# A diffusion-transformer layer on one core: two more 1 MB slots for streamed weights, and a 16-float load on another queue

## The chip, the core and the metric

The kernel runs on one core of one Trainium2 chip. The core has a matrix engine (PE), a vector engine (DVE), a scalar engine (ACT), GpSimd (POOL) and a sync engine (SP) that here only issues transfers; every engine works through its own list of instructions in order. 16 DMA engines move data between device memory and the on-chip buffer (SBUF), which matmuls read; matmul results go to PSUM. The metric is the time of the whole layer on the device in microseconds (us).

## The reference

One layer over 512 tokens of width 1024, in float32: modulated RMSNorm, a projection to gated-MLP and attention inputs, chunked spatial gating, windowed attention with a sink, a gated merge, an output projection, and then a mixture of 16 experts in which each expert picks its 64 tokens.

```python
m = jnp.maximum(jnp.max(logits, axis=-1, keepdims=True), sink_l)      # sink: 16 floats, one a head
denom = jnp.sum(p, axis=-1, keepdims=True) + jnp.exp(sink_l - m)
...
h2 = modulate(rmsnorm(x, norm2_g[l]), sh2, sc2)
aff = jax.nn.softmax(h2 @ w_router, axis=-1)
top_w, top_idx = lax.top_k(jnp.swapaxes(aff, 1, 2), 64)               # 64 tokens for each of 16 experts
xe = h2[top_idx]
y = (silu(xe @ w_gate) * (xe @ w_up)) @ w_down                        # 3 x 8 MB of weights an expert
x = x + g2 * scatter_add(y * top_w)
out = rmsnorm(x, final_g)
```

## The kernel before

Tokens lie on partitions in four tiles of 128. The source fixes the order on every engine (`manual_schedule`); a framework adds the waits. Large data lives in `NW` = 24 slots of 1 MB (`W()`, 128 partitions of 2048 floats); a new tile takes a slot whose last reader is done, and its writer waits for that reader. Small tiles are `S()` (6 of 512 floats a partition), PSUM tiles `B()` and `B2()`.

**The start** (lines 115 to 475). SP issues, in order: a table, `x`, parameter rows, the first half of `w_ada` in 8 transfers (`load_ada(0)`), the first piece of `w_in`, `ctx`, parameter rows, `load(1)` (1 MB), `load_ada(1)` (8 of 0.5 MB), and the mask and rotation table `tab` (line 409, 832 KB). SP keeps eight transfers under way, each on one of eight semaphores in turn: a transfer is issued when the one eight before it has landed. The attention sink (16 floats, to all partitions, 8 KB) is loaded on POOL's queue (line 133) and negated on DVE (line 134), the second instruction of DVE's list. DVE, ACT and PE then turn `x` by features (lines 400 to 404) and multiply the condition with `w_ada` (`mod_rows`, line 278); `mod_cols(0)` copies that result (DVE, line 284), turns it (PE, line 288) and makes scale and shift; `mod_x(0)` applies them (DVE line 303, ACT line 304), and the first products of the projection (`mm3`, lines 110 to 112) follow on PE.

**The middle** (to about 590 us) is a row of such products, attention and the merge. The sink is read there, from line 570 on.

**The experts.** Each expert's weights come in 24 pieces of 1 MB (8 gate, 8 up, 8 down), 384 in all, in one order (`stream`); `stream_to(n)` issues them up to number n. In the last projection it is called with 13 and 15, before the top-64 search with `ring[0]` = NW - 2 = 22 (two slots hold the residual rows `acc`), and then in `take(i)`, which allows pieces up to i + `ring[0]`. At the first expert's piece 8, `settle()` takes three slots out of the ring: two for the normed rows `xn` (ACT, line 1189) and one, `g2w`, for a gate row and transposed hidden values; from there on a piece goes to the slot that was freed 19 pieces earlier. For the first expert the rows are gathered from the raw rows `xacc` with a one-hot matrix that carries the norm's factor (`gather_first`); the others gather from `xn` (`gather`, line 1124). `up_half` does gate and up on PE (line 1211), `down` the rest (line 1250). The rows of the expert before are added to `xacc` in `up_half` after pieces 1 and 4 (`add_rows`, PE line 1265, DVE line 1272). After the last expert come the last additions, the norm and four stores.

Of the kernel before, what the change touches and what calls it, by code (L numbers as in the profile page):

```python
# [5 lines left out]
F32 = mybir.dt.float32  # L6
F32R = mybir.dt.float32r
AF = mybir.ActivationFunctionType
ALU = mybir.AluOpType
# [3 lines left out]
P = 128  # L13
D = 1024
T = 512
NT = 4
CT = 2
KD = 8
H = 16
G = 4  # L20
DH = 64
E = 16
# [1 line left out]
DE = 2048  # L24
EPS = 1e-6
NEG = -1e30
NW = 24

TAB_MASK = 0
TAB_C = 1152  # L30
# [40 lines left out]
def bc_rows(ap1d, n):  # L71
    return bass.AP(tensor=ap1d.tensor, offset=ap1d.offset, ap=[[0, P], [1, n]])


def layer(tc, I, out, dbg=None):
    nc = tc.nc
    pe, act, dve, gp, sp = nc.tensor, nc.scalar, nc.vector, nc.gpsimd, nc.sync
    from contextlib import ExitStack
    with ExitStack() as st:
        cp = st.enter_context(tc.tile_pool(name="cp", bufs=1))  # L80
        big = st.enter_context(tc.tile_pool(name="big", bufs=NW))
        sm = st.enter_context(tc.tile_pool(name="sm", bufs=6))
# [5 lines left out]
        def W(dt=F32):  # L88
            return big.tile([P, 2048], dt, name="w")

        def S(dt=F32):
            return sm.tile([P, 512], dt, name="s")

        def V(n=4):
            t = tiny.tile([P, 16], F32, name="v")
            return t[:, :n]

        def B(dt=F32):
            return psb.tile([P, 512], dt, name="b")

        def B2():
            return ps2.tile([P, 1024], F32, name="b2")
# [27 lines left out]
        vT = cp.tile([P, C_N], F32, name="vT")  # L130
        modT = cp.tile([P, 16, 2], F32, name="modT")
        sink = cp.tile([P, H], F32, name="sink")
        gp.dma_start(sink, bc_rows(I["attn_sink"][0], H))
        dve.tensor_scalar(sink, sink, -1.0, None, ALU.mult)


        win = I["w_in"][0]
# [75 lines left out]
        for i in range(2):  # L213
            for j in range(2):
                t = 2 * i + j
# [7 lines left out]
        def load_ada(h):  # L223

            for i in range(4):
                w = W()
                for j in range(2):
                    k = 2 * i + j
                    wv = w[:, j * D:(j + 1) * D].rearrange("p (m c) -> p m c", m=2)
                    src = I["w_ada"][0, k * P:(k + 1) * P, 0:2048].rearrange("p (m a c) -> a p m c", m=2, a=2)[h]  # L230
                    sp.dma_start(wv, src)
                ada[h, i] = w
# [38 lines left out]
        def mod_rows(h, i):  # L271

            if i == 0:
                pms[h] = b2m[:, :512] if h else B()
            for m in range(2):
                for j in range(2):
                    o = 32 * (2 * j + m)
                    pe.matmul(pms[h][o:o + 32, :], sT[:, 2 * i + j, :], ada[h, i][:, j * D + m * 512:j * D + (m + 1) * 512],
                              start=(i == 0), stop=(i == 3))
# [117 lines left out]
        for k in range(KD):  # L397
            p = B()
# [8 lines left out]
        load(1)  # L407
        load_ada(1)
        sp.dma_start(tab[:, :TAB_IOTA], I["tab"][:, :TAB_IOTA])

        mod_rows(0, 3)
        for _ in range(2):
# [272 lines left out]
        for a in range(2):  # L685
            p = B()
# [67 lines left out]
        sh2c, a2c, g2c = [cp.tile([P, KD], F32, name=n) for n in ("sh2c", "a2c", "g2c")]  # L754
# [56 lines left out]
                dve.tensor_tensor(wr, wr, a2c[:, :, None].to_broadcast([P, KD, E]), ALU.mult)  # L811
                dve.tensor_reduce(part, wt.rearrange("p k e -> p e k"), axis=AX.X, op=ALU.add)

        part = cp.tile([P, E], F32, name="part")

        def shift_logits():
            ones = S()[:, :P]
# [16 lines left out]
        for side in range(2):  # L834
            yh, yl = (yah, yal) if side == 0 else (ybh, ybl)
            for c in range(4):
# [5 lines left out]
                for u_ in range(4):  # L842
                    f = 2 * c + u_ % 2
                    wh, wl = tiles[i0 + u_]
                    p = B()
# [15 lines left out]
                    else:  # L861
                        z = zs[u_ - 2]
                        m = mA[f // 4][:, (f % 4) * T:(f % 4 + 1) * T]
# [29 lines left out]
        ew = {}  # L893
        ring = [NW - 2]
        issued = [0]
# [12 lines left out]
        xacc = lambda t: acc[t // 2][:, (t % 2) * D:(t % 2 + 1) * D]  # L908
        for t in range(NT):
            sp.dma_start(xacc(t), I["x"][0, t * P:(t + 1) * P, :])  # L910
        xnw = []
        xn = lambda t: xnw[t // 2][:, (t % 2) * D:(t % 2 + 1) * D]
        rstd2 = cp.tile([P, NT], F32, name="rstd2")
        aff = cp.tile([P, NT, E], F32, name="aff")
        def out_cols(t, c0, n, hooks):

            p = B()[:, :n]
            for k in range(KD):
                wh, wl = split_done[30 + c0 // 512 * 2 + k // 4]
                c = slice(c0 % 512, c0 % 512 + n)  # L920
                mm3(p, mgh(k)[:, t * P:(t + 1) * P], mgl(k)[:, t * P:(t + 1) * P], wh[:, k % 4, c], wl[:, k % 4, c],
                    k == 0, k == KD - 1)
                if k + 1 in hooks:
                    hooks[k + 1]()
            return p
# [35 lines left out]
                dve.tensor_copy(XT[t, c0][:, :n], p[:, :n])  # L961

        strips = {}
        pos = cp.tile([P, NT, E], F32, name="pos")
        fold = pos[:, 0]
        dve.tensor_reduce(fold, idt.rearrange("p (j c) -> p c j", j=4)[:, :E], axis=AX.X, op=ALU.add)

# [57 lines left out]
        for i, (t, c0, n) in enumerate(units):  # L1025
            before = units[i - 1] if i else None
# [3 lines left out]
            p = out_cols(t, c0, n, hooks)  # L1030
# [41 lines left out]
        def one_hot(e, scale=None):  # L1072
            oh = S()[:, :512].rearrange("p (t s) -> p t s", t=NT)
            for t in range(NT):
                o = oh[:, t].rearrange("p (h s) -> p h s", h=2)
                if scale is None:
                    dve.tensor_scalar(o, iota, pos[:, t, e:e + 1], None, ALU.is_equal)  # L1077
                else:
                    dve.tensor_scalar(o, iota, pos[:, t, e:e + 1], scale[:, t:t + 1], ALU.is_equal, ALU.mult)
            return oh  # L1080
# [36 lines left out]
                to_modulated(0, pt[a], ks, a * 256)  # L1117

        def gather(e):
            oh = one_hot(e)  # L1120
            p = B()
            for t in range(NT):
                for h in range(2):
                    pe.matmul(p[h * 64:(h + 1) * 64, :], oh[:, t, :64], xn(t)[:, h * 512:(h + 1) * 512],  # L1124
                              start=(t == 0), stop=(t == NT - 1))
            XE[e] = p, oh

        def gather_turn(e):
# [10 lines left out]
        def gather_rest(e):  # L1139

            xt, ohv = XE[e]
            if e == 0:
                ohv = one_hot(e)
            pw = B()
            for t in range(NT):
                pe.matmul(pw[:, :1], ohv[:, t], aff[:, t, e:e + 1], start=(t == 0), stop=(t == NT - 1))  # L1146
            tw = V(1)
            dve.tensor_copy(tw, pw[:, :1])
            pt_ = B()
            for t in range(NT):  # L1150
                pe.transpose(pt_[:, t * P:(t + 1) * P], ohv[:, t], idt)
            oht = S()
            act.activation(oht[:, :512], pt_, AF.Copy)
            XE[e] = (xt, tw, oht)

        g2w = []

        def diag_rows(cols, a, w):

            ones = S()[:, :w]  # L1160
            gp.memset(ones, 1.0)  # L1161
            dg = S()
            gp.tensor_tensor(dg.rearrange("p (k c) -> p k c", k=4), idt[:, None, :].to_broadcast([P, 4, P]),
                             cols[:, a * 4:a * 4 + 4, None].to_broadcast([P, 4, P]), ALU.mult)
            return ones, dg
# [9 lines left out]
        def spread_halves(o, cols):  # L1175

            p = B()
            for a in range(2):
                ones, dg = diag_rows(cols, a, 64)
                pe.matmul(p[a * 64:(a + 1) * 64, :], ones, dg, start=True, stop=True)  # L1180
            dve.tensor_copy(o, p)

        def settle():

            xnw.extend([W(), W()])
            g2w.append(W())
            ring[0] -= 3
            for t in range(NT):
                act.activation(xn(t), xacc(t), AF.Copy, scale=rstd2[:, t:t + 1])
            spread_halves(g2w[0][:, :512], g2c)  # L1190

        def take(i):
            if i == KD:
                settle()
            stream_to(i + ring[0])
            return ew.pop(i)

# [2 lines left out]
        def up_half(e, before):  # L1200
            xt = XE[e][0]
            pp_ = []
            for m in range(2):
                p = B2()
                pp_.append(p)
                for k in range(KD):
                    w = take(e * 24 + m * 8 + k)
                    x = xt[:, k % 4, k // 4, :]
                    for n in range(2):
                        for h in range(2):  # L1210
                            pe.matmul(p[h * 64:(h + 1) * 64, n * 512:(n + 1) * 512], x,  # L1211
                                      w[:, h * D + n * 512:h * D + (n + 1) * 512],
                                      start=(k == 0), stop=(k == KD - 1))
                    if before and m == 0 and k in (1, 4):
                        add_rows(*before, (0, 1) if k == 1 else (2, 3))
            hs = []
            for n in range(2):
                s = S()
                act.activation(s[:, :512], pp_[0][:, n * 512:(n + 1) * 512], AF.Silu)  # L1219
                dve.tensor_tensor(s[:, :512], s[:, :512], pp_[1][:, n * 512:(n + 1) * 512], ALU.mult)  # L1220
                hs.append(s)
            HT[e] = hs
# [45 lines left out]
        def add_rows(e, yw, ts):  # L1268
            ps = put_back(e, yw, ts)
            for (t, c), p in ps.items():  # L1270
                x = xacc(t)[:, c * 512:(c + 1) * 512]
                dve.tensor_tensor(x, x, p, ALU.add)  # L1272
# [67 lines left out]
```

## Time and profile before

| what | us |
|---|---|
| median of 3 runs (1558.88 to 1560.78) | 1559.96 |
| the profiled execution, its own time | 1560.64 |
| its span, first to last instruction | 1558.9 |
| PE busy | 1441.8 (92%) |
| DVE / ACT / POOL busy | 530.4 / 317.2 / 124.2 |
| bytes moved | 474.15 MB, mean 304 GB/s |

The profile shows one execution on a time axis that starts with its first instruction. A busy PE says little by itself, since matmuls are pipelined; what matters in a stretch is who waits for whom there.

### The profile page before, as it was taken

Reading aid. Unit: us, or ns where it says so; the run is one execution under the profiler, and the core shown is the slowest. Engines: PE = TensorE matmul, PEld = TensorE weight load, DVE = VectorE, ACT = ScalarE, POOL = GpSimd, SP = SyncE. Lnnn points to the kernel's source line nnn. Section 1 sums busy time; section 2 is a strip of 40 time slices with the busy share of each in tenths; the row PEclk is TensorE's granted clock in tenths of the full one; section 3 lists DMA queues with packets and bytes.
Section 4 is the critical chain, followed back from the end, with each engine's and each line's share of the span. In section 5 each row is a group of like instructions: output and inputs, shape, how many; then the busy total and the mean of one; then the engine's idle time right before and its main releaser. Section 6 shows DMA issues by size and latency. Waiting matters only on the chain.

```text
span 1558.9 us, 18259 instructions
## 1 busy us (share of the span) xinstructions
PE 1441.8 (92%) x7471; PEld 764.7 (49%) x7471; DVE 530.4 (34%) x1079; ACT 317.2 (20%) x605; POOL 124.2 (8%) x184
## 2 busy tenths in 40 slices
PE   5899999999999997999999999989989889889895
PEld 3687787788788884333333333323323323323221
DVE  4666555468664335112112121211211112112123
ACT  4456555533232331200000000000000000000002
POOL 2143322000000321000000000000000000000002
PEclk9999999999999998999999999999999999999998
DMA  9310000437762666999999999999999999999994
GB/s 330 127 55 28 28 28 28 136 106 251 254 174 82 240 246 273 374 412 420 420 419 420 420 420 419 419 420 420 420 420 419 420 419 419 420 419 419 420 420 183
DMA packets 99272, 474.15 MB, mean 304 GB/s; under 512 B 8842, under 2 KB 38770, under 8 KB 47986
## 3 DMA queue, kind: packets, MB, share of 16 engines
q1 hardware_dynamic: 99156, 472.97, 76.3%
q8 instruction: 59, 0.97, 0.3%
q0 software_dynamic: 32, 0.01, 0.1%
q14 instruction: 25, 0.20, 0.0%
HBM read 470.85 MB, written 2.10 MB: 303 GB/s over the span
## 4 chain that ended last, share of the span: by engine, by line
PE 73%; issue 14%; DMA 5%; DVE 5%; ACT 3%; SPq 0%; POOL 0%; POOLq 0%; ACTq 0%; DVEq 0%
PE b L1211 15%; PE b L1250 13%; PE b L110 8%; PE b L112 8%; PE b L111 8%; PE b L1265 4%; PE b L1124 4%; PE b L610 3%; PE b L617 2%; DMA w<-in_w_exp_up_dram 1%; DMA w<-in_w_exp_gate_dram 1%; DMA w<-in_w_exp_down_dram 1%; DVE s L1220 1%; PE b L1232 1%; PE b L1146 1%
## 5 line engine op out<-in xcount | busy, mean ns | idle before, releaser
L1211 PE MATMUL b<-w,s 128*64 128x512 f32 x2048 | 460.6, 596 | 28.8 <-DMA w<-in_w_exp_up_dram 28.8
L1211 PEld LDWEIGHTS b<-w,s 128*64 128x64 f32 x2048 | 139.0, 137 | 343.3 <-issue 256.6
L110 PE MATMUL b<-w 128*128 128x512 f32 (+1 forms) x720 | 257.2, 357 | 2.7 <-ACT w L304 2.7
L112 PE MATMUL b<-w 128*128 128x512 f32 (+1 forms) x720 | 247.6, 344 | 0.0
L111 PE MATMUL b<-w 128*128 128x512 f32 (+1 forms) x720 | 247.3, 344 | 0.0
L1250 PE MATMUL b<-w 128*64 128x512 f32 x1024 | 227.9, 596 | 2.7 <-DMA w<-in_w_exp_down_dram 2.5
L110 PEld LDWEIGHTS b<-w 128*128 128x128 f32 x720 | 136.7, 190 | 34.6 <-issue 11.4
L112 PEld LDWEIGHTS b<-w 128*128 128x128 f32 x720 | 136.5, 190 | 16.7 <-DVE w L308 0.4
L111 PEld LDWEIGHTS b<-w 128*128 128x128 f32 x720 | 136.9, 190 | 15.3 <-issue 0.2
L1250 PEld LDWEIGHTS b<-w 128*64 128x64 f32 x1024 | 70.2, 137 | 137.6 <-issue 128.6
L1220 DVE TENSOR_TENSOR s<-s,b 128x512 f32<-128x512 f32 x32 | 20.6, 684 | 312.3 <-issue 285.1
L1272 DVE TENSOR_TENSOR w<-w,b 128x512 f32<-128x512 f32 x128 | 79.5, 682 | 128.3 <-PE b L1265 128.3
L1219 ACT ACTIVATE s<-b 128x512 f32<-128x512 f32 x32 | 17.4, 594 | 343.3 <-PE b L1211 343.3
L107 POOL TENSOR_TENSOR w<-w 128x512 fp32r<-128x512 f32 x52 | 67.3, 1308 | 194.0 <-ACT w L106 185.7
L106 ACT ACTIVATE w<-w 128x512 fp32r<-128x512 f32 (+2 forms) x97 | 79.9, 848 | 8.5 <-DVE w L315 5.0
L1235 ACT ACTIVATE w<-b 128x512 f32<-128x512 f32 x16 | 9.6, 597 | 335.6 <-PE b L1232 335.6
L1124 PE MATMUL b<-w,s 128*64 128x512 f32 x240 | 54.8, 598 | 24.7 <-DVE s L1077 24.7
L1161 POOL MEMSET s<- 128x64 f32 (+1 forms) x4 | 0.7, 180 | 872.6 <-PE b L1135 850.2
L571 DVE CUSTOM_DVE_ANT_0 w<-b,w,sink 128x512 f32<-128x512 f32 (+1 forms) x64 | 51.5, 813 | 52.7 <-PE b L567 52.4
L1265 PE MATMUL b<-s 64*128 64x512 f32 x256 | 65.0, 616 | 1.8 <-DVE w L1272 1.0
L107 DVE TENSOR_TENSOR w<-w 128x1024 fp32r<-128x1024 f32 (+1 forms) x45 | 58.0, 1293 | 24.8 <-ACT w L106 24.8
L583 ACT ACTIVATE w<-w,v 128x513 f32<-128x513 f32 (+1 forms) x64 | 49.0, 769 | 0.0
(223 smaller groups left out, 1110.2 us busy)
## 6 DMA issues: line engine op xcount, KB each, us to landing
w<-in_w_exp_gate_dram SPq DMA_DIRECT2D x128, 1024.0 KB, 19.9
w<-in_w_exp_up_dram SPq DMA_DIRECT2D x128, 1024.0 KB, 19.9
w<-in_w_exp_down_dram SPq DMA_DIRECT2D x128, 1024.0 KB, 19.9
w<-in_w_in_dram SPq DMA_DIRECT2D x21, 1024.0 KB, 5.1
w<-in_w_ada_dram SPq DMA_DIRECT2D x16, 1024.0 KB, 5.0
w<-in_w_ada_dram SPq DMA_DIRECT2D x16, 512.0 KB, 6.0
w<-in_x_dram SPq DMA_DIRECT2D x8, 512.0 KB, 6.1
w<-in_w_proj_a_dram SPq DMA_DIRECT2D x4, 1024.0 KB, 5.2
```

The source lines that it names most:

```text
L106: act.activation(hi, raw, AF.Copy)
L107: eng.tensor_tensor(lo, raw, hi.bitcast(F32), ALU.subtract)
L110: pe.matmul(o, sh, mh, start=first, stop=False)
L111: pe.matmul(o, sh, ml, start=False, stop=False)
L112: pe.matmul(o, sl, mh, start=False, stop=last)
L571: dve.tensor_tensor_reduce(s[:, :w_], p[:, 256:256 + w_], mask[:, c0:c0 + w_], -1.0, sk, ALU.add, ALU.min, mx[:, r:r + 1])
L583: act.activation(sm_t[r][:, :w_], sm_t[r][:, :w_], AF.Exp, bias=mx[:, r:r + 1], scale=-1.0, accum_out=den[:, r:r + 1])
L1124: pe.matmul(p[h * 64:(h + 1) * 64, :], oh[:, t, :64], xn(t)[:, h * 512:(h + 1) * 512], start=(t == 0), stop=(t == NT - 1))
L1211: pe.matmul(p[h * 64:(h + 1) * 64, n * 512:(n + 1) * 512], x, w[:, h * D + n * 512:h * D + (n + 1) * 512], start=(k == 0), stop=(k == KD - 1))
L1250: pe.matmul(y[c * 64:(c + 1) * 64, :], hT[n][:, i % 2, j, h, :], w[:, j * D + c * 512:j * D + (c + 1) * 512], start=(i == 0 and j == 0), s ...
L1265: pe.matmul(ps[t, c], XE[e][2][r, t * P:(t + 1) * P], yw[r, :], start=True, stop=True)
L1272: dve.tensor_tensor(x, x, p, ALU.add)
```

## The change

The buffer of big slots grows from 24 to 26; room comes from a smaller DMA scratch area of GpSimd (64 bytes) and from `part`, which becomes a piece of `pos`. GpSimd issues no transfer any more: the sink is loaded by SP, behind `tab`, and its negation stands at that place of the source. The three slots of `settle` are taken in two steps: `g2w` at piece 8, as before, and the two for `xn` at piece 26, the third of the second expert. So the second expert too is gathered from `xacc` with a scaled one-hot matrix, and `gather_rest(1)` makes a plain one. `add_rows` comes after pieces 3 and 6, so that the rows are copied before they are changed.

```diff
-NW = 24
+NW = 26
...
-        gp.dma_start(sink, bc_rows(I["attn_sink"][0], H))
-        dve.tensor_scalar(sink, sink, -1.0, None, ALU.mult)
...
         load_ada(1)
         sp.dma_start(tab[:, :TAB_IOTA], I["tab"][:, :TAB_IOTA])
+        sp.dma_start(sink, bc_rows(I["attn_sink"][0], H))
+        dve.tensor_scalar(sink, sink, -1.0, None, ALU.mult)
 
         mod_rows(0, 3)
...
-        part = cp.tile([P, E], F32, name="part")
+        pos = cp.tile([P, NT, E], F32, name="pos")
+        part = pos[:, 1]
...
         def gather(e):
-            oh = one_hot(e)
+
+            oh = one_hot(e, None if xnw else rstd2)
+            rows_ = xn if xnw else xacc
...
-                    pe.matmul(p[h * 64:(h + 1) * 64, :], oh[:, t, :64], xn(t)[:, h * 512:(h + 1) * 512],
+                    pe.matmul(p[h * 64:(h + 1) * 64, :], oh[:, t, :64], rows_(t)[:, h * 512:(h + 1) * 512],
                               start=(t == 0), stop=(t == NT - 1))
+            if not xnw:
+                oh = None
             XE[e] = p, oh
...
-            if e == 0:
+            if ohv is None:
                 ohv = one_hot(e)
...
         def take(i):
             if i == KD:
-                settle()
+                settle_gate()
+            if i == 3 * KD + 2:
+                settle_rows()
             stream_to(i + ring[0])
...
-                    if before and m == 0 and k in (1, 4):
-                        add_rows(*before, (0, 1) if k == 1 else (2, 3))
+                    if before and m == 0 and k in (3, 6):
+                        add_rows(*before, (0, 1) if k == 3 else (2, 3))
...
-    nc = bacc.Bacc("TRN2", target_bir_lowering=False, num_devices=1)
+    nc = bacc.Bacc("TRN2", target_bir_lowering=False, num_devices=1, dynamic_dma_scratch_size=64)
```

DVE near the start, before: the sink is negated first, on POOL's transfer semaphore (DMASW0), and the copy of line 284 follows the four copies of turned `x`.

```order
L124 CAST idr<-tab_76 128x128 [waits DMAHW0_49]
L134 TENSOR_SCALAR sink<-sink 128x16 [waits DMASW0_49]
L248 TENSOR_SCALAR v<-v 128x1 [waits Activation_49] x2
...
L404 COPY w<-b 128x512 [waits PE_49] x4
L284 COPY s<-b 128x512 [waits PE_49]
L294 TENSOR_TENSOR modT<-b,vT 128x2x4 [waits DVE_49,PE_49]
```

Now (lines have moved up by two at this place):

```order
L124 CAST idr<-tab_76 128x128 [waits DMAHW0_49]
L246 TENSOR_SCALAR v<-v 128x1 [waits Activation_49] x2
...
L402 COPY w<-b 128x512 [waits PE_49] x4
L409 TENSOR_SCALAR sink<-sink 128x16 [waits DMAHW4_49]
L282 COPY s<-b 128x512 [waits PE_49]
L292 TENSOR_TENSOR modT<-b,vT 128x2x4 [waits DVE_49,PE_49]
```

The negation has moved from the second place of DVE's list to one directly ahead of the copy of `mod_cols(0)`, and it waits for a transfer of SP (DMAHW4). On SP the list has one row more, behind `tab`; before:

```order
L231 DMA w_248<-in_w_ada_dram 128x2x512 [waits DMAHW1_49]
L231 DMA w_248<-in_w_ada_dram 128x2x512 [waits DMAHW2_49]
L409 DMA w_75<-in_tab_dram 128x1664 [waits DMAHW3_49]
L177 DMA w_384<-in_w_in_dram 128x8x256 [waits DMAHW4_49,DVE_49,PE_49]
L177 DMA w_483<-in_w_in_dram 128x8x256 [waits DMAHW5_49,DVE_49]
```

and now:

```order
L229 DMA w_246<-in_w_ada_dram 128x2x512 [waits DMAHW1_49]
L229 DMA w_246<-in_w_ada_dram 128x2x512 [waits DMAHW2_49]
L407 DMA w_75<-in_tab_dram 128x1664 [waits DMAHW3_49]
L408 DMA sink_89<-in_attn_sink_dram 128x16 [waits DMAHW4_49]
L175 DMA w_384<-in_w_in_dram 128x8x256 [waits DMAHW5_49,PE_49]
L175 DMA w_483<-in_w_in_dram 128x8x256 [waits DMAHW6_49,PE_49]
```

The sink stands behind `tab` and in the place that a piece of `w_in` had in the turn of the semaphores; the two pieces of `w_in` behind it no longer wait for DVE.

## Rows read from the trace of the kernel before

**Rows 1.** Page, part 2: 40 slices of 39 us; busy tenths, and GB/s moved.

```profile
PE   5899999999999997999999999989989889889895
DMA  9310000437762666999999999999999999999994
GB/s 330 127 55 28 28 28 28 136 106 251 254 174 82 240 246 273 374 412 420 420 419 420 420 420 419 419 420 420 420 420 419 420 419 419 420 419 419 420 420 183
```

**Rows 2.** PE's timeline: start, length, instruction, count, idle before and what ended it.

```profile
1536.75 1.94 PE L1250 MATMUL b<-w 128*64 128x512 f32 x8 [0.54 <-DMA w<-in_w_exp_down_dram]
```

**Rows 3.** Stretches of 10 us: busy time of each engine, clock, DMA share, GB/s.

```profile
570.00:580.00 10.00, 10.00 (x87) 10.00 (x86) 2.79 (x9) 2.69 (x9) 0.00 (x0) 1.00 0.14 59
580.00:590.00 10.00, 10.00 (x88) 10.00 (x87) 4.31 (x17) 3.49 (x13) 1.65 (x3) 1.00 0.08 11
...
610.00:620.00 10.00, 8.96 (x61) 4.95 (x62) 4.40 (x15) 0.98 (x4) 2.33 (x4) 1.00 0.35 125
620.00:630.00 10.00, 10.00 (x48) 3.30 (x46) 0.00 (x0) 0.00 (x0) 0.00 (x0) 1.00 0.93 351
...
650.00:660.00 10.00, 9.23 (x52) 4.48 (x50) 3.94 (x15) 1.57 (x3) 0.00 (x0) 1.00 0.80 301
660.00:670.00 10.00, 10.00 (x54) 4.02 (x52) 0.16 (x1) 0.60 (x1) 0.00 (x0) 1.00 0.94 369
```

**Rows 4.** What SP's queue waited for, 525 to 690 us: total, times, longest.

```profile
SPq L900 <- PE b L1211: 58.5, 21, 22.5
SPq L900 <- PE b L956: 26.8, 2, 26.6
SPq L900 <- PE b L1250: 20.7, 7, 9.6
```

**Rows 5.** PE's timeline, first expert and start of the second.

```profile
616.69 13.95 PE L1211 MATMUL b<-w,s 128*64 128x512 f32 x64
...
631.33 13.90 PE L1211 MATMUL b<-w,s 128*64 128x512 f32 x64
...
653.32 3.65 PE L1250 MATMUL b<-w 128*64 128x512 f32 x16
...
675.81 5.37 PE L1211 MATMUL b<-w,s 128*64 128x512 f32 x24
681.11 1.99 PE L1265 MATMUL b<-s 64*128 64x512 f32 x8
```

**Rows 6.** DVE's timeline: the sink, and the copy of `mod_cols(0)`.

```profile
7.27 0.17 DVE L134 TENSOR_SCALAR sink<-sink 128x16 f32<-128x16 f32 x1 [4.25 <-DMA sink<-in_attn_sink_dram]
...
24.83 0.69 DVE L284 COPY s<-b 128x512 f32<-128x512 f32 x1 [1.63 <-PE b L278]
```

**Rows 7.** SP's timeline (issues; a merged row's length includes its waits).

```profile
33.18 1.23 SPq L409 DMA_DIRECT2D w<-in_tab_dram  x1
34.58 14.65 SPq L177 DMA_DIRECT2D w<-in_w_in_dram  x3
```

**Rows 8.** Issues (the last: 34.5 to 36 us): count, KB, us from issue to landing.

```profile
w<-in_tab_dram SPq DMA_DIRECT2D x1, 832.0 KB, 13.0
sink<-in_attn_sink_dram POOLq DMA_DIRECT2D x1, 8.0 KB, 5.9
w<-in_w_in_dram SPq DMA_DIRECT2D x2, 1024.0 KB, 14.6
```

**Rows 9.** PE's timeline: the first product of the projection.

```profile
28.95 0.50 PE L110 MATMUL b<-w 128*128 128x512 f32 x1 [2.66 <-ACT w L304]
```

**Rows 10.** Stretches: PE, PEld, DVE, ACT, POOL busy, clock, DMA share, GB/s.

```profile
32.00:34.00 2.00, 2.00 (x6) 1.52 (x6) 1.90 (x4) 0.74 (x2) 0.21 (x1) 0.51 1.03 373
...
600.00:610.00 10.00, 8.81 (x31) 5.05 (x31) 9.48 (x20) 0.00 (x0) 0.00 (x0) 0.63 1.01 422
```

**Rows 11.** Timelines of ACT (normed rows) and DVE (scaled one-hot).

```profile
630.69 2.19 ACT L1189 ACTIVATE w<-w,rstd 128x1024 f32<-128x1024 f32 x2 [14.42 <-PE b L1211]
611.38 1.32 DVE L1079 TENSOR_SCALAR s<-tab,pos,rstd 128x128 f32<-128x128 f32 x4 [0.71 <-ACT pos L1067]
```

More of the change, by code (lines that the diff above doesn't have):

```diff
@@ L963, in layer @@
         strips = {}
-        pos = cp.tile([P, NT, E], F32, name="pos")
         fold = pos[:, 0]
@@ L1181, in spread_halves, with settle_gate, settle_rows @@
             dve.tensor_copy(o, p)
-        def settle():
+        def settle_gate():
+            g2w.append(W())
+            ring[0] -= 1
+            spread_halves(g2w[0][:, :512], g2c)
+        def settle_rows():
             xnw.extend([W(), W()])
-            g2w.append(W())
-            ring[0] -= 3
+            ring[0] -= 2
             for t in range(NT):
                 act.activation(xn(t), xacc(t), AF.Copy, scale=rstd2[:, t:t + 1])
-            spread_halves(g2w[0][:, :512], g2c)
         def take(i):
             if i == KD:
-                settle()
+                settle_gate()
+            if i == 3 * KD + 2:
+                settle_rows()
             stream_to(i + ring[0])
```

## The prediction

> **What bounds the kernel now.** I read the page's slices first [rows 1]. From slice 17 (some 660 us) to the end the DMA engines move 419 to 420 GB/s in every slice. Before that PE is at nine tenths or more in all slices but the first two and the one of the top-64 search (7), and the DMA rate is lower. So the kernel has two parts: up to the first expert PE sets the pace, and in the experts the transfer of the weights does. A piece of 1 MB takes 1.0486 MB / 420 GB/s = 2.50 us, the 384 pieces 959 us. That the end hangs on this stream is shown by the last products [rows 2]: PE idles until the last piece of `down` has landed, at 1536.75, and the remaining 22 us (additions, norm, stores) follow from that.
>
> So two things count: when the first expert starts on PE (616.69 [rows 5]), and how many pieces are in by then and how steadily the rest follows. The stretches of 10 us [rows 3] show where the DMA engines were not full after the stream's start. From 570 to 590 they nearly rest (59 and 11 GB/s), and around 612 to 626 again. In 650 to 670 they run at 301 and 369 GB/s: against 420 that is 2.8 + 1.2 = 4.0 us of lost transfer. The table of SP's waits [rows 4] says why: issues wait for PE, that is for slots (26.6 us before the projection's end, then for the first expert's products). From 670 on nothing is lost.
>
> **Part 1: two more slots.** Before, 22 pieces are in when the first expert starts; pieces 22 to 28 take the slots of pieces 0 to 6, and from piece 29 on a piece needs the slot freed 19 earlier. Now 24 are in; the two more are loaded in the idle 570 to 590, where 18 us were free for 5.0 us of work. The following pieces need the slot freed 24 earlier, from piece 31 on 23, from piece 48 on 21. When the first expert starts, loading begins in both kernels with piece 0's slot, free at 616.69 + 13.95/8 = 618.4 [rows 5]. Counted from there, 360 pieces are left instead of 362: 2 x 2.50 = 5.0 us gained.
>
> Does the hole at 650 to 670 stay? Before, pieces 22 to 34 were in at 654, and piece 35 needed piece 16's slot, the first of `down`, which PE frees at 653.32 + 3.65/2 = 655.1 [rows 5]. Now, from the same 654, pieces 24 to 36 are in, and piece 39 is the one that needs piece 16's slot: it is due when 37 and 38 are in, at 659.0, 3.9 us after that slot is free. The hole closes: 4.0 us. The next narrow place is the second expert, where 21 slots are left: piece 48 needs piece 27's slot, free at about 677.4 (the row at 675.81 [rows 5] holds pieces 26 to 28, 1.8 us each; without the additions ahead of it, some 2 us as in the row at 681.11, it starts at 673.8), and is due at 681.5. Piece 49 needs piece 28's, free 1.99 us of additions and one piece later, at some 681, and is due at 684.0: 3 us ahead. Later PE frees slots faster (1.74 us a piece) than they fill. In sum 9.0 us of gain. Bounds: 5.0 if the hole only moves, and 9.6, with 0.6 of the slow restart at 620 to 630 (351 GB/s, 1.6 us lost [rows 3]) saved too. I take 9.0, as every place worked out has a margin.
>
> PE does not become the bound instead: it stands still for transfers in the last expert [rows 2], and the stream now leads by only 9 us more.
>
> **Part 2: rows made at the second expert.** The gather reads raw instead of normed rows, of the same shape and type: nothing on PE. The scaled one-hot takes 1.32/4 = 0.33 us a tile [rows 11], a few tenths ahead of PE's gather in one expert. The second one-hot of `gather_rest(1)` lies on DVE while PE does `down`. ACT's four copies (2 x 2.19 us [rows 11]) move to the second expert, where ACT has nothing else; they end before the additions that change those rows. All of this lies under a PE that has slack against the stream: 0, bounds 0 and 0.5.
>
> **Part 3: the sink on SP.** Before, the sink landed 5.9 us after POOL issued it [rows 8], and DVE negated it at 7.27 [rows 6], before there was anything else to do. That goes; DVE then waits for `x` anyway: 0. Now the negation stands on DVE directly ahead of the copy of `mod_cols(0)`, which started at 24.83, when PE's products were done [rows 6]. And its transfer stands on SP behind `tab`, which SP issued at 33.18, with the next issue at 34.58 [rows 7]; this next place is the sink's. So DVE, which works in order, stands at the negation from about 24.8 until the sink has landed. Behind it is queued all that leads to the projection: the copy, PE's transposes, scale and shift, `mod_x`, and PE's first product, 28.95 [rows 9]. ACT and POOL wait for the same chain.
>
> When does the sink land? The nearest rows: `tab`, just ahead, lands 13.0 us after its issue, at 46.2; the next piece of `w_in`, just behind, 14.6 us after 34.58, at 49.2 [rows 8]. Between the two lie 3.0 us, hardly more than the 2.5 us of that piece alone, so transfers land in the order of issue. A transfer of 8 KB between them should land just behind `tab`: 46.5. With 0.2 for the negation (0.17 [rows 6]) the copy starts at 46.7 instead of 24.83: 21.9 us late. Bounds: 34.58 + 5.9 = 40.5 (the price of the same 8 KB on POOL's queue), which makes 15.9, and 49.2, which makes 24.6. I take 21.9, since the sink's place in the queue is nearest to `tab`.
>
> The Trainium skill bears on that order in "DMA: Bandwidth & Descriptors", section "Queues, rings and completion order": a transfer's semaphore increment lands only after every earlier write of the same DMA engine. By that rule the landings of `tab` and of the piece behind it agree with the row, and the sink could not be seen before `tab` is in.
>
> Is a late start absorbed? What comes between it and 590 us is PE at nine tenths and more [rows 1], in chains that hang on each other; no slack takes up 20 us. The transfers of that stage only come earlier against PE. The stream's issues wait for slots that this stage frees, so they move with it. I count the delay in full: the first expert starts 21.9 us later.
>
> There is one more term. PE rests some 25 us instead of 4. In the start before, 32 to 34 was granted 0.51, about the lower of its two levels (1.2 of 2.4 GHz) [rows 10], after the gap that ended at 28.95 [rows 9]. Behind PE's longer rest in the top-64 search, 600 to 610 runs at 0.63 [rows 10], which over 10 us is 3.7 us of full clock missing, part of it while PE rests. I take 0.8 for a lower level that holds on longer behind the longer rest, bounds 0 and 1.7, and cannot show it closer.
>
> **Sum.** 1560.64 (the profiled execution's own time) + 21.9 + 0.8 - 9.0 = 1574.3. That execution lies 0.7 above the median of 1559.96: 1573.7.
>
> **Rivals.**
> *The sink lands early.* A transfer this small may get through before `tab` has wholly landed. For it: on POOL it needed only 5.9 us with `x` under way. Against it: the order of landings above. It would then be 40.5, a delay of 15.9: 1559.96 + 15.9 + 0.8 - 9.0 = 1567.7.
> The Trainium skill has a page for the extreme of this, "DMA: Bandwidth & Descriptors", section "Anatomy of one DMA": 2.0 us of fixed cost and the bytes at 436 GB/s. As an estimate from it, an idle queue would have the sink in at 36.6 and the kernel at 1563.8; the rows of `tab` and `w_in` (13.0 and 14.6 us for less than 3 us of bytes) speak against a queue that is idle.
> *The slots bring less.* If the hole of 650 to 670 reappears at the second expert (21 slots, margins of 3 to 4 us), or pieces released one by one load at the lower rate of 620 to 630, 5.0 or less is left of the gain: 1577.7; with none of it 1582.7.
> *Faster.* The change does at the start what it does in the experts only if DVE does not stand: the sink would have to be in before 24.83 + 9.0 = 33.8, from where on the two slots outweigh the delay. Place: DVE's negation; price: nothing; time: 1551.0. SP would have to issue the sink before its row of 33.18, though eight transfers under way hold it back to there. Little speaks for it.
>
> **How the numbers follow.** Chances: my forecast (1570.5 to 1577, from 2.5 us about the landing and 1 us about clock and hole) 0.78; the early sink (1563.5 to 1570) 0.10; the slots bring less (1577 to 1583) 0.07; faster 0.05. The range 1567 to 1578.5 holds the first and about half of the second and a third of the third. About 0.2%, 3.1 us, is what a measurement of this kernel can tell from no change; nearly all of the cases lie above 1563.1. So slower 0.94, within 0.01, faster 0.05.
>
> **What would show it.** Right: on DVE a wait of about 22 us ahead of the negation, ended by the sink's transfer; PE's first product at 51 instead of 28.95; the first expert's first product near 639 (616.69 + 22.7); no stretch under 400 GB/s behind 650 + 22.7; and 911 us from that first product to the last piece's landing, 9.0 less than 1536.75 - 616.69 = 920.1. Wrong: a negation before 34; a hole in the stream in the second expert; or a first expert that starts less late than the projection's first product, which would mean that the middle does absorb.

## The result, and the profile after

The changed kernel takes 1569.28 us (median of 4 runs, 1568.59 to 1570.71) beside 1559.42 for the kernel before (4 runs): a ratio of 1.0066, with a 95% interval of 1.0053 to 1.0079. It is slower, by 9.9 us; 1573.7 was forecast, with 1567 to 1578.5 as range. Its profiled execution took 1570.71 us (span 1568.9), beside 1560.64 and 1558.9 of before.

DVE's timeline near the start, after the change (start, length, instruction, in brackets the idle time ahead and what ended it), answers [rows 6]:

```profile
44.49 0.18 DVE L409 TENSOR_SCALAR sink<-sink 128x16 f32<-128x16 f32 x1 [23.20 <-DMA sink<-in_attn_sink_dram]
44.57 0.68 DVE L282 COPY s<-b 128x512 f32<-128x512 f32 x1
```

DVE stands for 23.2 us at the negation until the sink has landed, and the copy behind it starts at 44.57 instead of 24.83, 19.74 us later. Its cause stands on SP, in the timeline of its issues and in the table of issues of 33 to 37 us (KB each, us from issue to landing), which answer [rows 7, 8]:

```profile
31.76 0.61 SPq L407 DMA_DIRECT2D w<-in_tab_dram  x1
33.11 0.35 SPq L408 DMA_DIRECT2D sink<-in_attn_sink_dram  x1
34.53 5.55 SPq L175 DMA_DIRECT2D w<-in_w_in_dram  x2
```

```profile
sink<-in_attn_sink_dram SPq DMA_DIRECT2D x1, 8.0 KB, 11.4
```

The sink is issued at 33.11 and is 11.4 us under way, for 8 KB. PE's timeline shows what hangs on it (first products of the projection, and the 36th; first expert; second expert with the first additions; last piece of `down`), as in [rows 2, 5, 9]:

```profile
45.40 1.09 PE L286 MATMUL b<-tab,s 128*128 128x128 f32 x4 [22.55 <-DVE s L282]
48.54 0.79 PE L110 MATMUL b<-w 128*128 128x512 f32 x1 [2.05 <-ACT w L302]
...
58.56 0.39 PE L112 MATMUL b<-w 128*128 128x512 f32 x1
...
635.88 13.95 PE L1221 MATMUL b<-w,s 128*64 128x512 f32 x64
...
689.62 7.04 PE L1221 MATMUL b<-w,s 128*64 128x512 f32 x32
696.59 1.99 PE L1275 MATMUL b<-s 64*128 64x512 f32 x8
...
1546.94 1.94 PE L1260 MATMUL b<-w 128*64 128x512 f32 x8 [0.55 <-DMA w<-in_w_exp_down_dram]
```

The first product is 19.59 us late against [rows 9], the first expert 19.19 against [rows 5], the last piece 10.19 against [rows 2]. So 19.2 us are lost before the experts, and 9.0 come back within them: 1546.94 - 635.88 = 911.06 us, where it was 920.06. Where they come back, stretches of 10 us show (columns as in [rows 10]: busy time of PE, PEld, DVE, ACT and POOL, then the granted clock as a share of TensorE's full clock, the DMA share, GB/s), as in [rows 3]:

```profile
590.00:600.00 10.00, 10.00 (x87) 10.00 (x87) 2.72 (x9) 2.43 (x9) 0.00 (x0) 1.00 0.02 10
600.00:610.00 10.00, 9.99 (x85) 9.78 (x84) 4.08 (x18) 3.49 (x13) 1.65 (x3) 1.00 0.11 21
...
640.00:650.00 10.00, 10.00 (x48) 3.32 (x46) 0.00 (x0) 0.08 (x1) 0.00 (x0) 1.00 1.01 406
...
660.00:670.00 10.00, 8.21 (x39) 2.73 (x36) 2.31 (x6) 0.00 (x0) 0.00 (x0) 1.00 1.02 419
670.00:680.00 10.00, 9.23 (x52) 4.57 (x53) 4.72 (x19) 1.57 (x3) 0.00 (x0) 1.00 1.01 419
680.00:690.00 10.00, 10.00 (x53) 3.95 (x50) 0.25 (x2) 0.60 (x1) 0.00 (x0) 1.00 1.02 417
...
700.00:710.00 10.00, 10.00 (x48) 3.18 (x44) 2.77 (x5) 1.08 (x2) 0.00 (x0) 1.00 0.98 388
710.00:720.00 10.00, 10.00 (x50) 3.37 (x48) 0.00 (x0) 0.00 (x0) 0.00 (x0) 1.00 1.01 413
...
730.00:740.00 10.00, 10.00 (x54) 4.09 (x52) 1.93 (x9) 0.13 (x1) 0.00 (x0) 1.00 1.00 401
```

All of it lies 19 us later than before. The hole of 301 and 369 GB/s, which would now be at 670 to 690, is gone. What is left are dents of 388, 413 and 401 at 700 to 740, where the second expert runs with 21 slots; against 420 they cost 1.4 us. SP still waits as long as before for slots. In the table of its waits (total, times, longest), over the stretch of [rows 4] moved by 19 us (544 to 709), the first expert's products stand with 57.8 us where [rows 4] has 58.5; but these waits no longer empty the DMA engines:

```profile
SPq L901 <- PE b L1221: 57.8, 21, 21.8
SPq L901 <- PE b L957: 26.8, 2, 26.6
```

The second row, the longest wait ahead of the projection's end, is unchanged too, and so is the pause of the DMA engines that goes with it (10 and 21 GB/s at 590 to 610, 59 and 11 in [rows 3]). The two more pieces were therefore not loaded in that pause, as forecast, but ahead of it: the 35 us ahead of the pause moved 409 GB/s instead of 372. And in the first 10 us of the first expert the stream restarts a little faster, at 256 instead of 220. These two stretches, in the kernel before and then in the changed one:

```profile
536.69:571.69 35.00, 35.00 (x223) 29.05 (x222) 13.20 (x26) 12.96 (x29) 13.06 (x11) 1.00 0.93 372
616.69:626.69 10.00, 10.00 (x49) 3.43 (x50) 1.71 (x7) 0.00 (x0) 0.28 (x1) 1.00 0.67 220
```

```profile
555.88:590.88 35.00, 35.00 (x224) 29.06 (x223) 12.99 (x26) 13.08 (x29) 12.82 (x11) 1.00 0.99 409
635.88:645.88 10.00, 10.00 (x49) 3.45 (x50) 1.71 (x7) 0.00 (x0) 0.28 (x1) 1.00 0.69 256
```

The change is thus two changes: a gain of 9 us among the experts and a loss of 19 us at the start. One more thing in the trace was not foreseen: the start itself runs faster up to the stall. The copy's input was ready some 2 us sooner than before, which experiment 3 is about.

### The profile page after: what moved, and what is told of

Its sections match the earlier page's. It is cut to its first block, busy times and chain, and to the rows that moved or that the text cites. A ratio compares the mean times of both kernels' runs of the same rounds, so it can differ in the third digit from the quotient of the medians.

```text
span 1568.9 us, 18291 instructions
## 1 busy us (share of the span) xinstructions
PE 1439.7 (92%) x7471; PEld 766.2 (49%) x7471; DVE 532.1 (34%) x1083; ACT 316.8 (20%) x605; POOL 123.4 (8%) x183
## 4 chain that ended last, share of the span: by engine, by line
PE 66%; DMA 17%; issue 10%; DVE 4%; ACT 2%; POOL 0%; SPq 0%; POOLq 0%; ACTq 0%; DVEq 0%
PE b L1221 13%; PE b L1260 11%; PE b L110 8%; PE b L112 8%; PE b L111 8%; DMA w<-in_w_exp_gate_dram 5%; DMA w<-in_w_exp_down_dram 5%; DMA w<-in_w_exp_up_dram 4%; PE b L1275 3%; PE b L1126 3%; PE b L610 3%; PE b L617 2%; DVE s L1230 1%; PE b L564 1%; PE b L567 1%
## 5 line engine op out<-in xcount | busy, mean ns | idle before, releaser
L110 PEld LDWEIGHTS b<-w 128*128 128x128 f32 x720 | 136.6, 190 | 34.0 <-issue 11.4
L1230 DVE TENSOR_TENSOR s<-s,b 128x512 f32<-128x512 f32 x32 | 20.6, 684 | 254.0 <-issue 226.9
## 6 DMA issues: line engine op xcount, KB each, us to landing
w<-in_w_exp_gate_dram SPq DMA_DIRECT2D x128, 1024.0 KB, 19.9
w<-in_w_exp_up_dram SPq DMA_DIRECT2D x128, 1024.0 KB, 19.9
w<-in_w_exp_down_dram SPq DMA_DIRECT2D x128, 1024.0 KB, 19.9
```

Source lines behind the costliest of these rows:

```text
L110: pe.matmul(o, sh, mh, start=first, stop=False)
```

## The experiments

Theory: the loss is DVE's in-order wait at the negation, for a sink that stands behind `tab` in SP's queue; the slots and the split settling are a gain that hardly depends on it. The rivals were: the loss comes from the sink's load on SP, wherever its reader stands; the gain needs all parts of the change at once, or the split gives nothing; the transfer that left POOL's queue matters. Times are medians, ratios those to the kernel before, run on the same chip, with 95% intervals.

**1. The negation alone moved.** The changed kernel, with the negation behind the last key tile, still ahead of the sink's first reader:

```diff
         sp.dma_start(sink, bc_rows(I["attn_sink"][0], H))
-        dve.tensor_scalar(sink, sink, -1.0, None, ALU.mult)
...
             key_tile(kt)
 
+        dve.tensor_scalar(sink, sink, -1.0, None, ALU.mult)
 
         QT = {}
```

> The changed kernel with one line moved: the negation of the sink stands behind the last key tile, ahead of the queries, and not ahead of the copy of mod_cols(0). If the loss is DVE standing still for the sink's transfer (copy at 44.57 instead of about 22.9 in the changed kernel's trace), the 19.7 us between the two kernels' copies go: 1569.3 - 19.7 = 1549.6, give or take 1; DVE's copy near 23, PE's first product near 27, 911 us from the first expert's product to the last piece unchanged. If the loss lies elsewhere (other slots, other waits in the middle), it stays above 1560.

Measured: 1548.67 us, 0.9933 (0.9920 to 0.9947). DVE's copy, in its timeline:

```profile
22.27 0.69 DVE L282 COPY s<-b 128x512 f32<-128x512 f32 x1 [1.63 <-PE b L276]
```

The transfer is the same and takes about as long (12.1 us); only nobody waits for it. One line's place is worth some 20 us (1569.28 - 1548.67 = 20.6), and the load on SP costs nothing by itself. This version is faster than both kernels.

**2. The sink's change alone, with 24 slots.** Two kernels: the kernel before with the sink's load and negation where the change puts them, and the same with the negation late. The slots and the settling stay as before.

```diff
-        gp.dma_start(sink, bc_rows(I["attn_sink"][0], H))
-        dve.tensor_scalar(sink, sink, -1.0, None, ALU.mult)
...
         sp.dma_start(tab[:, :TAB_IOTA], I["tab"][:, :TAB_IOTA])
+        sp.dma_start(sink, bc_rows(I["attn_sink"][0], H))
+        dve.tensor_scalar(sink, sink, -1.0, None, ALU.mult)
```

> The kernel before with the sink's move alone: loaded by SP behind the table, negated at that place, 24 slots and one settle step as before. DVE-stands theory: the copy of mod_cols(0) about 19.7 us later and all behind it with it, 1559.4 + 19.2 = 1578.6, give or take 1, and 920 us from the first expert to the last piece as before. If the middle absorbs part of a late start, or the delay needs the 26 slots, less: 1565 or below.

Measured: 1578.78 us, 1.0125 (1.0111 to 1.0138).

> The kernel before with the sink loaded by SP behind the table and negated behind the last key tile; 24 slots. Nothing waits for the sink, so only its absence from GpSimd's queue is left. If that transfer held up x at the start (87 to 106 GB/s in 4 to 6 us before, 377 to 401 in the changed kernel), x lands about 2 us earlier and everything follows: 1559.4 - 1.9 = 1557.5. If the slow stretch has another cause, or is made up before the projection: 1559.4, the same.

Measured: 1557.09 us, 0.9988 (0.9979 to 0.9997). The timelines of DVE, the first of the early negation, the second of the late one:

```profile
43.09 0.17 DVE L409 TENSOR_SCALAR sink<-sink 128x16 f32<-128x16 f32 x1 [22.70 <-DMA sink<-in_attn_sink_dram]
43.17 0.68 DVE L282 COPY s<-b 128x512 f32<-128x512 f32 x1
```

```profile
23.34 0.69 DVE L282 COPY s<-b 128x512 f32<-128x512 f32 x1 [1.63 <-PE b L276]
```

The loss of 19.9 us is there without the slots, and goes with the negation's place. Between the second of these kernels and that of experiment 1 lie only the slots, with the room made for them, and the settling, with the gather and the additions that go with it: 1557.09 - 1548.67 = 8.4 us, the gain forecast as 9.0. The other 1.8 us that the second one gains on the kernel before come from the sink's load having left POOL's queue, or from the negation having left the head of DVE's list. Experiment 3 tells these apart.

**3. Queue or negation.** The kernel before with one line moved: POOL still loads the sink, and DVE negates it late.

```diff
         gp.dma_start(sink, bc_rows(I["attn_sink"][0], H))
-        dve.tensor_scalar(sink, sink, -1.0, None, ALU.mult)
...
+        dve.tensor_scalar(sink, sink, -1.0, None, ALU.mult)
         QT = {}
```

> The kernel before with one line moved: the sink is still loaded from GpSimd's queue, but VectorE negates it only behind the last key tile. The kernel with the load on SyncE's queue and the same late negation began its first 16-column products 2.1 us earlier than the kernel before and was 1.8 us shorter. Theory A (the 8 KB transfer on GpSimd's queue holds up the loads of x beside it): the second square of ScalarE still starts near 8.5 us, the copy of the first adaLN row on VectorE near 24.8, and the time is that of the kernel before, ratio 1.000 (within 0.0008). Theory B (the negation at 7.27 us, waiting for its load, held VectorE's queue and with it the row norms): the square starts near 6.5, the copy near 23.1, and the time is 1.6 to 1.9 us shorter, ratio 0.9988.

Measured: 1559.11 us beside 1559.06, 1.0002 (0.9993 to 1.0011). It is the queue: the kernel of experiment 2 with the same late negation, but with the load on SP, stood at 0.9988. ACT's timeline (the second square of `x`), two stretches of 1 us, and the DMA queues of 3 to 6 us (packets, MB, share of 16 engines) of this kernel:

```profile
8.60 1.03 ACT L255 ACTIVATE b<-w 128x1024 f32<-128x1024 f32 x1 [2.16 <-DMA w<-in_x_dram]
```

```profile
4.00:5.00 1.00, 0.00 (x0) 0.00 (x0) 0.00 (x0) 0.00 (x0) 0.00 (x0) 1.00 0.77 115
5.00:6.00 1.00, 0.00 (x0) 0.00 (x0) 0.00 (x0) 0.71 (x1) 0.00 (x0) 1.00 1.01 102
```

```profile
q1 hardware_dynamic: 145, 0.53, 50.1%
q0 software_dynamic: 22, 0.01, 38.8%
```

The same views of the changed kernel, which has nothing on POOL's queue:

```profile
6.51 1.03 ACT L254 ACTIVATE b<-w 128x1024 f32<-128x1024 f32 x1
```

```profile
4.00:5.00 1.00, 0.00 (x0) 0.00 (x0) 0.00 (x0) 0.00 (x0) 0.00 (x0) 1.00 0.98 377
5.00:6.00 1.00, 0.00 (x0) 0.00 (x0) 0.00 (x0) 0.78 (x1) 0.00 (x0) 1.00 1.05 401
```

```profile
q1 hardware_dynamic: 304, 1.12, 99.9%
```

With POOL's transfer (q0) under way, the engines are busy but move 102 to 115 GB/s instead of 377 to 401, and the second square starts 2 us later, after a wait for its tile of `x`. Its 22 packets took 38.8% of 16 engines over 3 us, 0.85 us each; SP's took 50.1%, 0.17 us each (145 packets). The kernel before shows the same (22 packets with 40.5%). The Trainium skill says in "DMA: Bandwidth & Descriptors", section "Queues, rings and completion order", that each DMA engine takes turns between the queues it has work for, a whole packet at a time. The rows agree with that: slow packets of one queue hold the other one up. That the turns are the cause is read from these rows and was not tested apart. Why these packets are slow no run here shows.

**4. The sink issued early.** The changed kernel with the negation where the change puts it, but the sink issued ahead of `load(1)` and `load_ada(1)` instead of behind `tab`:

```diff
+        sp.dma_start(sink, bc_rows(I["attn_sink"][0], H))
         load(1)
         load_ada(1)
         sp.dma_start(tab[:, :TAB_IOTA], I["tab"][:, :TAB_IOTA])
-        sp.dma_start(sink, bc_rows(I["attn_sink"][0], H))
         dve.tensor_scalar(sink, sink, -1.0, None, ALU.mult)
```

> The changed kernel with the sink's transfer issued ahead of load(1) and load_ada(1) instead of behind the table; the negation stays ahead of the copy of mod_cols(0). Order-of-issue theory: at 24.5 us little is under way (62 to 188 GB/s), the sink lands within 2 to 3 us, the copy starts at about 27 instead of 44.6, and the kernel takes 1569.3 - 17.4 = 1552 (1550.5 to 1555). If the 11.4 us from issue to landing belong to this kind of transfer (64 bytes a partition) wherever it stands: landing at 36, copy 8.6 us earlier than in the changed kernel, 1560.7.

Measured: 1554.22 us, 0.9970 (0.9959 to 0.9982). The issue and the wait, in the table of issues (22 to 25 us) and in DVE's timeline:

```profile
sink<-in_attn_sink_dram SPq DMA_DIRECT2D x1, 8.0 KB, 3.8
```

```profile
27.30 0.17 DVE L409 TENSOR_SCALAR sink<-sink 128x16 f32<-128x16 f32 x1 [6.08 <-DMA sink<-in_attn_sink_dram]
```

Issued at 23.45, where the transfers ahead of it were nearly through, the same 8 KB land in 3.8 us, a little more than the 2 to 3 expected. The stall shrinks from 23.2 to 6.1 us and the kernel is 15 us shorter than the changed one. So the price of the wait is set by what stands ahead in the queue; but as long as it stands in front of the copy it costs what is left of it: 5.6 us against experiment 1.

**5. Slots and settling apart.** The kernel of experiment 1 with the settling in one step at piece 8 and the additions after pieces 1 and 4, as before, so that it has only the two slots (and the sink's late negation); and the kernel before with only the split settling, the raw gather of the second expert and the additions after 3 and 6, with 24 slots and the sink as it was. For the first:

```diff
             if i == KD:
-                settle_gate()
-            if i == 3 * KD + 2:
-                settle_rows()
+                settle()
...
-                    if before and m == 0 and k in (3, 6):
+                    if before and m == 0 and k in (1, 4):
```

> The kernel of e1_late_negation (26 slots, sink negated late) with the three slots taken in one step at piece 8 and the additions after pieces 1 and 4, as before: the two more slots alone. Sum of the prediction: pieces 24 to 36 are in when piece 37 needs the slot of piece 16, so the hole of 4.0 us in the stream stays, some 55 us behind the first expert's product, and only the 5.0 us of two more pieces are gained: 1548.7 + 4.0 = 1552.7, and 915 us from the first expert's product to the last piece instead of 911. Rival: the slots alone close the hole, and the split is worth nothing: 1548.7.

> The kernel before with 24 slots and the sink on GpSimd's queue, but with the slots taken in two steps (one at piece 8, two at piece 26), the second expert gathered from the raw rows and the additions after pieces 3 and 6. Sum of the prediction: the hole at 650 to 670 us closes, 4.0 us: 1558.9 - 4.0 = 1554.9, and 916 us from the first expert's product to the last piece instead of 920. Rival: with fewer slots the hole only moves to the second expert, or the gather from raw rows costs what the hole gives back: 1558.9.

Measured: 1551.98 us, 0.9938 (0.9924 to 0.9951), and 1555.03 us, 0.9968 (0.9952 to 0.9983). From the first expert's first product to the last piece the traces show 914.5 and 916.2 us. But the runs of the kernel before spread from 1557.98 to 1564.02 beside these two, so that the first could not be told from the 0.9933 of experiment 1. All three were run again beside each other.

> The kernel with the late negation once more (26 slots, rows normed at the second expert, sink on SyncE, negated behind the last key tile), timed beside the one-step and the split-alone kernel. Theory (its trace: 911.1 us from the first expert product to the last piece): 0.9934 of the kernel before; the rival, that the time over whole runs doesn't follow the traces, would put it level with the one-step kernel, at 0.995.

> 26 slots with the settling in one step at piece 8, sink on SyncE, negated late, once more. Theory (its trace: 914.5 us from the first expert product to the last piece, a hole of about 250 GB/s-10us at 650 to 670): 3.4 us longer than the late-negation kernel beside it, 0.9956 of the kernel before. Rival (the split of the settling is worth nothing): level with the late-negation kernel, 0.9934.

> 24 slots and the sink as in the kernel before, with the split settling, the second expert gathered from raw rows and the additions behind pieces 3 and 6, once more. Theory (its trace: 916.2 us from the first expert product to the last piece, no hole behind 650): 3.8 us shorter than the kernel before, 0.9975. Rival (it gives nothing alone): 1.000.

Measured, beside 1559.06 of before:

| kernel | us | ratio | first expert to last piece, us |
|---|---|---|---|
| both, negation late | 1548.50 | 0.9933 (0.9920 to 0.9947) | 1524.36 - 612.99 = 911.37 |
| 26 slots, one step | 1552.80 | 0.9959 (0.9947 to 0.9972) | 1529.02 - 614.08 = 914.94 |
| 24 slots, split | 1555.44 | 0.9978 (0.9969 to 0.9987) | 1532.93 - 617.21 = 915.72 |

Two stretches of each, in this order:

```profile
650.00:660.00 10.00, 10.00 (x52) 3.80 (x48) 3.63 (x17) 0.60 (x1) 0.00 (x0) 1.00 1.01 420
660.00:670.00 10.00, 10.00 (x54) 4.23 (x54) 0.91 (x2) 0.60 (x1) 0.00 (x0) 1.00 1.01 417
```

```profile
650.00:660.00 10.00, 9.82 (x52) 4.17 (x53) 3.05 (x13) 0.78 (x2) 0.00 (x0) 1.00 0.82 304
660.00:670.00 10.00, 10.00 (x54) 4.04 (x52) 0.91 (x2) 0.60 (x1) 0.00 (x0) 1.00 0.99 385
```

```profile
650.00:660.00 10.00, 9.23 (x52) 4.50 (x50) 4.72 (x19) 1.58 (x3) 0.00 (x0) 1.00 1.01 421
660.00:670.00 10.00, 10.00 (x54) 3.97 (x52) 0.16 (x1) 0.60 (x1) 0.00 (x0) 1.00 1.01 419
```

The hole is there with 26 slots and one step, and gone with 24 slots and the split. So the split closes it. With 26 slots it is worth 3.6 us in the traces (914.94 - 911.37) and 4.3 in the medians, with 24 slots 4.3 (920.06 - 915.72) and 3.6. The slots bring the rest, 5.1 with the settling in one step (920.06 - 914.94) and 4.3 with the split (915.72 - 911.37), from the pieces that are in before the first expert. The smaller scratch area and the move of `part` came along with the slots; no run has them apart.

## Why the prediction was right, and where it was off

The direction, the range and the mechanism hold. Of what the prediction named to look for, the wait ahead of the negation (about 22 us; 23.2) and the 911 us from the first expert's product to the last piece (911.06) came out; PE's first product (48.54, where 51 was named) and the first expert's (635.88, where 639 was) are early with the smaller delay. One sign did not hold: a stretch behind the hole is under 400, the dent of 388 in the second expert.

The miss is 4.4 us, or 3.6 in the profiled executions (1574.3 against 1570.71). By terms:

- **The delay was over-sized: 21.9, measured 19.74** at the copy. The step that failed is "DVE then waits for `x` anyway: 0", the price of taking the sink off POOL's queue. That transfer slowed the loads of `x` beside it, and without it everything up to SP's issues runs 1.4 to 2 us earlier: `tab` is issued at 31.76 instead of 33.18, and the sink at 33.11 where 34.58 was assumed. Experiment 3 shows the queue as cause, at 1.8 us in the medians (0.9988 with the load on SP, 1.0002 with it on POOL). The row that should have raised the question was in the trace of before: ACT's second square waited for `x` for 2.3 us, while transfers moved 87 to 106 GB/s at 4 to 6 us. The rest is the landing, 11.4 us where 11.9 was assumed; it is within the spread of this transfer (10.5 to 12.1 in the kernels that issue it behind `tab`).
- **The order of landing was right.** The sink landed at 44.5, some 12.7 us after `tab` was issued; `tab` itself took 13.0 in [rows 8]. By that duration (the trace of after lists no landing of `tab`) it is about the moment at which `tab` was in. The rule that the prediction cites from the Trainium skill ("DMA: Bandwidth & Descriptors", section "Queues, rings and completion order"), by which a semaphore's increment lands only after the earlier writes of the same DMA engine, agrees with that. The rival of the early landing (a delay of 15.9) is out, and experiment 4 shows that it needs an emptier queue. The fit with 2.0 us of fixed cost that the prediction takes for an idle queue from the Trainium skill (the same page, section "Anatomy of one DMA") stands there for transfers that GpSimd issues. On SP's queue, with little ahead, experiment 4 measured 3.8 us.
- **The clock term of 0.8 was 0.** PE rested 22.55 us, most of it at a granted clock of 0.50, and began its products at that level; but from the first to the 36th it took 58.56 - 48.54 = 10.02 us, and 38.93 - 28.95 = 9.98 in the kernel before. There the clock fell during the first products, as the 0.51 in [rows 10] shows, and products 0.43 us apart went on to 33.9, 4.9 us after the first. After the change they went on to 52.5, 4.0 us after the first. Ahead of them the four transposes of the chain did take 1.09 us at 0.50, where they had taken 0.63, but the way from the copy to the first product did not get longer by it (48.54 - 44.57 = 3.97 us, before 28.95 - 24.83 = 4.12). On the path the longer rest cost nothing more.
- **"Absorbed: nothing" was right within 0.6:** of 19.74 us at the copy, 19.59 are left at the first product and 19.19 at the first expert. To the letter the 0.4 between the last two is the sign of a middle that absorbs; but beside the kernel of experiment 1 (first product 26.82, first expert 613.80) it is the other way round, 21.72 and 22.08.
- **The gain of 9.0 was right in size, but credited to the wrong part, and its terms came out with some luck.** Part 1 called it the slots', and Part 2 gave the split 0. In fact its working took the split in silently, with "from piece 31 on 23". With two slots and one step, piece 37 would need piece 16's slot, 21 earlier, and be due at 654 when that slot comes free at 655.1, as late as in the kernel before. With 24 slots and the split it is piece 37 too, but due two pieces later, at 659. Experiment 5 shows just this: 4.3 to 5.1 for the slots, 3.6 to 4.3 for the split. The place of the slots' term was wrong as well: the two pieces were loaded ahead of the pause at 570 to 590 and not in it, since SP had no slot to issue to there. And two terms that the sum had at 0 nearly cancel: in the first 10 us of the first expert 256 GB/s instead of 220 gave 0.9 us, and the dents in the second expert, where margins of 3 to 4 us were worked out, took 1.4. That the rows of the second expert cost nothing holds: PE's additions at 696.59 follow its products at 689.62 without a wait.

So the sum should have been 21.9 - 2.2 (mostly the queue), 0 for the clock and 9.0 of gain: 1559.42 + 19.7 - 9.0 = 1570.1, 0.8 from the 1569.28 measured.

## What to carry to other kernels

A tiny load can take as long as a large one: here 8 KB landed about when the 832 KB ahead of them in the queue had landed. So the instruction that first waits for it belongs as late in its engine's list as its readers allow, above all when that list leads to the critical chain. When a load moves from one queue to another, look at what shares the time with it at the old place as well as the new. And when a change has several parts, work out each part's gain with the others undone, or the credit goes to the wrong one; here the whole was slower, although two of its three parts were gains and the third needs only one line moved.

## What the runs showed of the hardware

- One transfer of 8 KB on POOL's queue, 64 bytes to a partition, held the loads on SP's queue to 102 to 115 GB/s for 2 us, with its packets at 0.85 us of an engine each against 0.17 of SP's. Taking it away gave 1.8 us.
- The same 8 KB on SP's queue took 3.8 us with little ahead of them, and 10.5 to 12.1 behind 0.5 to 1 MB loads, in five kernels.
- A longer rest of TensorE cost its products no more than a short one: with a last rest of 2.66 us [rows 9] the granted clock fell to 0.51 during the first products, behind the rest of 22.55 us they began at 0.50; both times the first 36 products took 10.0 us.
